# RWKV-7, MoBA and dilated attention: small TensorE products in merged steps, dilated outputs straight to their two parts

## The chip, the cores and the metric

One core of one Trainium2 chip runs the whole program: TensorE (in the profile PE for its matmuls and PEld for its weight loads), VectorE (DVE), ScalarE (ACT), GpSimd (POOL) and SyncE (SP), which issues most of the DMAs. The metric is device microseconds of one execution. Of the kernel before there are three timed runs, and one profiled execution beside them.

## The reference, cut to what matters

Four mixers stand in a row in a network of width 1024 on 512 tokens, each followed by a layer norm and an MLP. The change is in the first mixer (RWKV-7 beside MoBA attention) and in the second (dilated attention).

```python
def step(S, inp):                      # RWKV-7, 8 heads of 64
    r_t, w_t, k_t, v_t, a_t, b_t = inp
    sa = jnp.einsum('bhvk,bhk->bhv', S, a_t)
    S = S * w_t[:, :, None, :] + sa[..., None] * b_t[:, :, None, :] + v_t[..., None] * k_t[:, :, None, :]
    return S, jnp.einsum('bhvk,bhk->bhv', S, r_t)
...
p = jax.nn.softmax(s_all, axis=-1)     # MoBA, 4 heads of 128: with 2 blocks of 256 it is causal attention
...
for g, (span, dilation) in enumerate(((128, 1), (512, 4), (2048, 16))):   # dilated, 8 heads of 128
    o, l = _dilated_window_branch(q[:, g], k, v, span, dilation)
...
o = jnp.einsum('gbht,gbhtd->bhtd', wts, jnp.stack(outs, axis=0))
return o.reshape(B, T, C_WIDTH) @ w_out
```

The decay and the gates of RWKV-7 come from products with small matrices (`w_up`, `a_up`, `g_up`), and its output is normed by head, scaled and gated.

## The kernel before, in words

All matrices of weights are multiplied as two fp32r parts (a rounded value and what is left of it), three matmuls of 512 columns each: `gemm` in lines 276 to 278, `pjps` in lines 361 to 363. Everything small (all that the change touches in the first mixer) is in plain fp32, where each matmul of the program shows as two instructions in the trace.

The first mixer fills the first 355 us. RWKV-7 works on pairs of heads, p = 0 to 3, in chunks of 64 tokens (c = 0, 1 in each of four tiles t of 128 tokens). For each pair four generators make the work: `prep` (decay, keys, transposes to token order), `inner` (products within the chunks: `aak`, `arb`, `ark`), `core` (the inverse of a triangular matrix by doubling, then `tu`, the chunk's transition `mt` and contribution `ct`, the states, the output `yk`) and `tail` (norm and gate). MoBA has one generator per head. A small product takes a part of TensorE's array, given by `tile_position`: (64·h, 64·c) is the quarter of 64 rows and 64 columns that reads partitions 64·h and writes partitions 64·c.

The order of the work is made by a planner, `race`. Each generator yields (TensorE time, time until its result can be used) in estimated microseconds after each step; the planner takes the step that is ready first, and between steps it deals out triples of the big products from `stream`: after each step it owes 0.65 of that step's TensorE time in triples (`RACE_RWKV`), and pays as soon as over 0.6 us is owed. After that the framework's scheduler lays out each engine's queue, roughly in that order, and puts in all waits. The engines' queues run in order.

PSUM has eight banks. Two hold the big products. The other six are one ring (`K.mps`) for all small products of all generators: a step takes a bank when its matmuls start and gives it back when ACT or DVE has read it out.

In the steps that the change touches, the kernel before handles the two heads of a pair, or the two halves c of the chunks, one after the other: one bank, 8 to 24 matmuls, a yield, then the read-out. Within such a step one of the two coordinates of `tile_position` stays the same, or both change together.

The dilated attention (790 to 1080 us) works through eight heads in a second planner run (`RACE_DIL`, 0.5), with a bank `po` for a head's whole output. At the head's end ACT copies `po` to `yT` in token order, and `split` makes the two fp32r parts of that head, `ys[0]` and `ys[1]`, which the out-projection (`early`) reads:

```python
nc.scalar.copy(yT[:, h, :].rearrange("p (t i r) -> p t r i", t=NT, r=4), po.rearrange("p (t r i) -> p t r i", t=NT, r=4))
at[0] = h + 1
yield 0, 0.6
K.split(ys[0][:, h], ys[1][:, h], yT[:, h])
```

Lines that the prediction speaks of: 472 and 478 (`pw`, `pa`), 452 (transposes), 564 (`pp` of `inner`), 591 (`pp` of `core`, 32 columns), 652 (`pg`), 663 (`ptu`), 680 to 682 (`pmc`), 698 (`pqt`), 737 (`py2`), 878 to 904 (MoBA), 1325 to 1327 (dilated output), 1277 (dilated scores) and 1770 (a product of another mixer that the change leaves alone).

Of the kernel before, what the change touches and what calls it, by code (L numbers as in the profile page):

```python
# [18 lines left out]
P = 128  # L19
T = 512  # L20
# [382 lines left out]
def rwkv(K, ctx, x, win, first, par_d, wup_d, gup_d, yT, heads, done, load, more):  # L403
# [61 lines left out]
    def prep(p, R):  # L465
# [11 lines left out]
        pa = K.mps("pa")  # L477
        nc.tensor.matmul(pa, lhsT=wup[64:128, cs], rhs=wa[64:128, :], start=True, stop=True)
        yield 0.85, 0.85
# [60 lines left out]
        for dst, src in ((bk, bt), (kk_tm, kt), (v_tm, zv)):  # L540
            ps = tmaj(src)
            yield 0.45, 0.6
            nc.scalar.copy(dst.rearrange("p t c -> p (t c)"), ps)
        R.update(at=at_, bt=bt, kt=kt, rt=rt, wc=wc, bk=bk, kk=kk_tm, v=v_tm)

    def inner(p, R, Z):

        while "v" not in R or p and not state.get(f"core{p - 1}"):
            yield None
        rhs = sp.tile([P, 8, 2, 64], F32, name="rhs")  # L550
        ps = tmaj(R["at"])
        yield 0.45, 0.6
        nc.scalar.copy(
            rhs.rearrange("p (h t) w v -> p t h w v", h=2)[:, :, :, 0, :], ps.rearrange("p (t h v) -> p t h v", t=NT, h=2)
        )
        Z["rhs"] = rhs
        for name, l, r, m in (("aak", "kt", "at", "mus"), ("arb", "bt", "rt", "mui"), ("ark", "kt", "rt", "mui")):
            o = sp.tile([P, 8, 64], F32, name=name)
            for h in range(2):
                ps = K.mps("pp")  # L560
                for t in range(NT):
                    for c in range(2):
                        s = slice(t * P + 64 * c, t * P + 64 * c + 64)
                        nc.tensor.matmul(
                            ps[64 * c : 64 * c + 64, 64 * t : 64 * t + 64], lhsT=R[l][64 * h : 64 * h + 64, s],
                            rhs=R[r][64 * h : 64 * h + 64, s], start=True, stop=True, tile_position=(64 * h, 64 * c),
                        )
                yield 0.65, 0.65
                nc.vector.tensor_tensor(
                    o[:, 4 * h : 4 * h + 4, :], ps[:, 0:256].rearrange("p (t c) -> p t c", t=NT),  # L570
                    cn(m).unsqueeze(1).to_broadcast([P, NT, 64]), op=ALU.mult,
                )
            Z[name] = o
            yield 0, 0.4

    def core(p, R, Z):
# [6 lines left out]
        for h in range(2):  # L583
            r = slice(64 * h, 64 * h + 64)
            ps = K.mps("pp32")
            for t in range(NT):
                for w in range(2):
                    for q in range(4):
                        i = t * P + 32 * q
                        j = i if w == 0 else t * P + 64 * (q // 2)  # L590
                        nc.tensor.matmul(
                            ps[32 * q : 32 * q + 32, 128 * w + 32 * t : 128 * w + 32 * t + 32], lhsT=at_[r, i : i + 32], rhs=bt[r, j : j + 32],
                            start=True, stop=True, tile_position=(64 * h, 32 * q),
                        )
            yield 1.1, 1.1
            pv = ps[:, 0:256].rearrange("p (w t c) -> p w t c", w=2, t=NT)
            nc.vector.tensor_tensor(a32[:, 4 * h : 4 * h + 4, :], pv[:, 0], cn("m32sl").unsqueeze(1).to_broadcast([P, NT, 32]), op=ALU.mult)
            nc.scalar.copy(a10[:, 4 * h : 4 * h + 4, :], pv[:, 1])
# [59 lines left out]
        for h in range(2):  # L658
            pt = K.mps("ptu").rearrange("p (t w v) -> p t w v", t=NT, w=2)
# [6 lines left out]
            yield 1.0, 1.0  # L666
# [7 lines left out]
        for c in range(2):  # L674
            r = slice(64 * c, 64 * c + 64)
            ps = K.mps("pmc").rearrange("p (w t v) -> p w t v", w=2, t=NT)
            for t in range(NT):
                for h in range(2):
                    o = slice(64 * h, 64 * h + 64)
                    nc.tensor.matmul(ps[o, 1, t], lhsT=bk[r, t, o], rhs=tu[r, 1, t, h], start=True, stop=False, tile_position=(64 * c, 64 * h))  # L680
                    nc.tensor.matmul(ps[o, 1, t], lhsT=kk_tm[r, t, o], rhs=v_tm[r, t, o], start=False, stop=True, tile_position=(64 * c, 64 * h))
                    nc.tensor.matmul(ps[o, 0, t], lhsT=tu[r, 0, t, h], rhs=bk[r, t, o], start=True, stop=True, tile_position=(64 * c, 64 * h))
            yield 1.9, 1.9
            nc.vector.tensor_tensor(ct[:, :, c, :], ps[:, 1], bc(wct[:, :, c], 64), op=ALU.mult)
            nc.scalar.copy(mt_[:, :, c, :], ps[:, 0])
# [7 lines left out]
        for c in range(2):  # L693
            r = slice(64 * c, 64 * c + 64)
            ps = K.mps("pqt")[:, 0:256].rearrange("p (t l) -> p t l", t=NT)
            for t in range(NT):
                for h in range(2):
                    nc.tensor.matmul(
                        ps[64 * h : 64 * h + 64, t], lhsT=tu[r, 0, t, h, :], rhs=arb[r, 4 * h + t, :], start=True, stop=True,
                        tile_position=(64 * c, 64 * h))  # L700
            yield 0.65, 0.65
            nc.vector.tensor_tensor(Q[:, :, c, :], ps, R["rt"].rearrange("p (t c l) -> p t c l", t=NT, c=2)[:, :, c], op=ALU.add)
# [29 lines left out]
        for h in range(2):  # L732
            r = slice(64 * h, 64 * h + 64)
            ps = K.mps("py2")[:, 0:256].rearrange("p (t v) -> p t v", t=NT)
            for t in range(NT):
                for c in range(2):
                    nc.tensor.matmul(
                        ps[64 * c : 64 * c + 64, t], lhsT=Q[r, t, c, :], rhs=st[r, 2 * t + c, :], start=True, stop=True,
                        tile_position=(64 * h, 64 * c))
            yield 0.65, 0.65  # L740
            nc.vector.tensor_tensor(yk[:, :, h, :], yk[:, :, h, :], ps, op=ALU.add)
# [4 lines left out]
    def tail(p, R):  # L746
# [27 lines left out]
        yield 0.45, 0.6  # L774
        yo = sp.tile([P, T], F32, name="yo", tag="sqy")
        nc.scalar.activation(yo, pyt, AF.Identity, scale=pc("lg", p), bias=pc("lb", p))
        pgt = K.mps("pgt")
        nc.tensor.matmul(pgt, lhsT=gup[:, 0, cs], rhs=wa_["zg0"], start=True, stop=False)
        yield 0.85, 0.85
        nc.tensor.matmul(pgt, lhsT=gup[0:32, 1, cs], rhs=wa_["zg1"][0:32], start=False, stop=True)  # L780
        nc.vector.tensor_tensor(yo, yo, yT[:, p, :], op=ALU.add)
        yield 0.85, 0.85
# [49 lines left out]
def moba(K, ctx, c0, rope_d, yT, done):  # L832
# [20 lines left out]
    def head(h, R):  # L853
# [15 lines left out]
        pv = K.mps("mopv")  # L869
        for t in range(NT):  # L870
            nc.tensor.transpose(pv[:, t * P : t * P + P], vt[:, t * P : t * P + P], ident)
        yield 0.45, 0.6
        nc.scalar.copy(v.rearrange("p t d -> p (t d)"), pv)
        pr = []
        for t in range(NT):
            n = P * (t + 1)
            ps = K.mps("mosc")
            nc.tensor.matmul(ps[:, 0:n], lhsT=q[:, t * P : n], rhs=k[:, 0:n], start=True, stop=True)
            yield 0.2 * (t + 1), 0.6
            nc.vector.tensor_tensor(ps[:, t * P : n], ps[:, t * P : n], K.c("caus"), op=ALU.add)  # L880
            st = s2.tile([P, 4], F32, name="mstat")
            nc.vector.tensor_reduce(st[:, 0:1], ps[:, 0:n], axis=AX.X, op=ALU.max)
            nc.vector.tensor_scalar(st[:, 1:2], st[:, 0:1], -scale, None, op0=ALU.mult)
            p_ = sp.tile([P, n], F32, name=f"mp{t}")
            yield 0, 0.6
            nc.scalar.activation(p_, ps[:, 0:n], AF.Exp, scale=scale, bias=st[:, 1:2], accum_out=st[:, 2:3])
            yield 0, 0.6
            nc.vector.reciprocal(st[:, 3:4], st[:, 2:3])
            nc.vector.tensor_scalar(p_, p_, st[:, 3:4], None, op0=ALU.mult)
            pr.append(p_)  # L890
        yT_ = yT[:, 4 + h, :]
        po = K.mps("mopo")
        for b in range(NT):
            n = T - P * b
# [3 lines left out]
            yield 0.11 * (NT - b), 0.4  # L898
            pT = s2.tile([P, T], F32, name="mpt")[:, 0:n]
            (nc.scalar.copy if b % 2 else nc.vector.tensor_copy)(pT, pt[:, 0:n])  # L900
            yield 0.6, 0.6
            nc.tensor.matmul(po[:, b * P : T], lhsT=v[:, b, :], rhs=pT, start=b == 0, stop=b == NT - 1)
            yield 0.2 * (NT - b), 0.4
# [311 lines left out]
def dilated(K, ctx, S, x, win, rope_d, yT, ys, w_out):  # L1215
# [42 lines left out]
    def head(h, L):  # L1258
# [25 lines left out]
        po = L.acc("dipo")  # L1284
        ps = score(0)
        yield 0.7, 0.8
        for t in range(NT):
# [10 lines left out]
            yield (0.9 if t < NT - 1 else 0), 0.9  # L1298
# [30 lines left out]
        yield 0, 0.6  # L1329
        K.split(ys[0][:, h], ys[1][:, h], yT[:, h])  # L1330
        have.add(h)

# [860 lines left out]
def program(tc, A):  # L2193

    nc = tc.nc
    with ExitStack() as top:
# [46 lines left out]
        with ExitStack() as c:  # L2243
# [154 lines left out]
```

## Time and profile before

| | |
|---|---|
| median of 3 runs | 2176.72 us (2176.64 to 2177.35) |
| the profiled execution | 2178.79 us, its span 2177.0 us |
| mean granted TensorE clock | 0.991 of full |
| PE busy | 2133.3 us, 98% |
| DVE busy | 1214.7 us, 56% |
| ACT busy | 791.9 us, 36% |
| POOL busy | 181.3 us, 8% |

The span runs from the first to the last instruction; the execution has 1.8 us around it. A busy PE is a PE with at least one matmul on its way: matmuls overlap, and a row of the timeline merges neighbouring instructions of one line into one row with their count. How long a group holds TensorE is therefore read from start to start.

### The profile page before, as it was taken

The page shows a single profiled execution, that of the slowest core. Times are in us where ns is not written, and L with a number is a line of the kernel's source. Part 1 is how long each engine was busy: PE and PEld are TensorE (multiplying, and loading weights), DVE is VectorE, ACT ScalarE, POOL GpSimd, SP SyncE. Part 2 cuts the span into 40 slices and gives each one's busy share as a digit, 9 for nine tenths or more (in the row PEclk, how much of TensorE's full clock was granted, in tenths as well). Part 3 has the DMA queues.
Part 4 walks back from the last instruction along what each step waited for, and adds up shares of the span by engine and source line. Part 5 has one row for each costly group of instructions (what it writes and reads, how often), then busy time and mean ns, then how long its engine had stood idle before and what let it go on. Part 6 is the DMA issues. An engine that isn't in the chain of part 4 may idle for free.

```text
span 2177.0 us, 37054 instructions
## 1 busy us (share of the span) xinstructions
PE 2133.3 (98%) x15646; PEld 1699.1 (78%) x15646; DVE 1214.7 (56%) x2406; ACT 791.9 (36%) x1289; POOL 181.3 (8%) x268
## 2 busy tenths in 40 slices
PE   8999999999999999999999999999999999999998
PEld 6666667888887888787788888878677779888887
DVE  6675666764444655555574444466756466344445
ACT  4332324523232354444352233235524354222222
POOL 0011010061035400000000000010010000000000
PEclk9999999999999999999999999999989999999999
DMA  4111114333333332222243233314211232232321
GB/s 145 41 51 41 40 41 175 107 117 97 102 106 105 96 127 78 71 75 78 91 142 91 91 99 97 97 43 145 65 50 39 87 107 98 96 97 96 98 87 39
DMA packets 56182, 193.18 MB, mean 89 GB/s; under 512 B 8208, under 2 KB 8720, under 8 KB 55504
## 3 DMA queue, kind: packets, MB, share of 16 engines
q1 hardware_dynamic: 52480, 184.50, 26.2%
q0 software_dynamic: 3536, 6.32, 0.9%
q8 instruction: 122, 2.00, 0.4%
q14 instruction: 44, 0.36, 0.1%
HBM read 182.37 MB, written 8.39 MB: 88 GB/s over the span
## 4 chain that ended last, share of the span: by engine, by line
PE 88%; DVE 6%; ACT 2%; DMA 2%; issue 1%; POOL 0%; SPq 0%; DVEq 0%; ACTq 0%
PE gemm L276 8%; PE mlpo L361 7%; PE mlpo L363 7%; PE mlpo L362 7%; PE gemm L277 7%; PE gemm L278 7%; PE mlps L248 5%; PE mlps L249 5%; PE mlps L250 5%; PE ffg L249 2%; PE ffg L250 2%; PE ffu L249 2%; PE ffg L248 2%; PE ffu L250 2%; PE ffu L248 2%; PE pjps L361 1%
## 5 line engine op out<-in xcount | busy, mean ns | idle before, releaser
L227 ACT CAST wh<-wr 128x1024 fp32r<-128x1024 f32 (+1 forms) x311 | 323.7, 1043 | 766.0 <-PE mlpo L363 247.8
L229 DVE TENSOR_TENSOR wl<-wr,wh 128x1024 fp32r<-128x1024 f32 (+1 forms) x308 | 375.6, 1221 | 373.4 <-ACT wh L227 279.4
L276 PE MATMUL gemm<-acth,wh 128*128 128x512 f32 (+1 forms) x672 | 304.1, 453 | 9.5 <-ACT acth L237 6.3
L361 PE MATMUL mlpo<-wh,mlph 128*128 128x512 f32 x688 | 270.9, 394 | 0.0
L277 PE MATMUL gemm<-actl,wh 128*128 128x512 f32 (+1 forms) x672 | 269.4, 401 | 0.0
L363 PE MATMUL mlpo<-wh,mlpl 128*128 128x512 f32 x688 | 269.3, 392 | 0.0
L278 PE MATMUL gemm<-acth,wl 128*128 128x512 f32 (+1 forms) x672 | 268.1, 399 | 1.1 <-DVE wl L229 1.1
L362 PE MATMUL mlpo<-wl,mlph 128*128 128x512 f32 x688 | 268.8, 391 | 0.0
L248 PE MATMUL mlps<-acth,wh 128*128 128x512 f32 x448 | 175.7, 392 | 0.0
L249 PE MATMUL mlps<-actl,wh 128*128 128x512 f32 x448 | 175.5, 392 | 0.0
L250 PE MATMUL mlps<-acth,wl 128*128 128x512 f32 x448 | 175.3, 391 | 0.0
L276 PEld LDWEIGHTS gemm<-acth,wh 128*128 128x128 f32 (+1 forms) x672 | 127.1, 189 | 55.7 <-issue 18.3
L363 PEld LDWEIGHTS mlpo<-wh,mlpl 128*128 128x128 f32 x688 | 129.2, 188 | 29.5 <-DVE mlpl L238 0.2
L278 PEld LDWEIGHTS gemm<-acth,wl 128*128 128x128 f32 (+1 forms) x672 | 127.2, 189 | 31.0 <-DVE wl L229 1.9
L362 PEld LDWEIGHTS mlpo<-wl,mlph 128*128 128x128 f32 x688 | 129.2, 188 | 28.3
L361 PEld LDWEIGHTS mlpo<-wh,mlph 128*128 128x128 f32 x688 | 129.4, 188 | 28.1 <-ACT mlph L237 0.4
L277 PEld LDWEIGHTS gemm<-actl,wh 128*128 128x128 f32 (+1 forms) x672 | 128.0, 190 | 22.4 <-issue 5.3
L1039 DVE SCALAR_TENSOR_TENSOR xres<-xres,mlpo 128x512 f32<-128x512 f32 x120 | 82.1, 685 | 110.4 <-PE mlpo L363 109.6
L250 PEld LDWEIGHTS mlps<-acth,wl 128*128 128x128 f32 x448 | 84.1, 188 | 18.9
L248 PEld LDWEIGHTS mlps<-acth,wh 128*128 128x128 f32 x448 | 84.2, 188 | 18.5
L249 PEld LDWEIGHTS mlps<-actl,wh 128*128 128x128 f32 x448 | 84.1, 188 | 18.3
L237 ACT CAST mlph<-mlp 128x512 fp32r<-128x512 f32 x86 | 53.3, 620 | 86.2 <-DVE mlp L1115 61.0
(619 smaller groups left out, 3660.2 us busy)
## 6 DMA issues: line engine op xcount, KB each, us to landing
wr<-mlp_w SPq DMA_DIRECT2D x128, 512.0 KB, 3.7
wr<-ffn_w SPq DMA_DIRECT2D x66, 512.0 KB, 3.5
wr<-c_w_in SPq DMA_DIRECT2D x40, 512.0 KB, 3.6
wr<-ab_w_in SPq DMA_DIRECT2D x25, 512.0 KB, 3.5
wr<-w_in SPq DMA_DIRECT2D x24, 512.0 KB, 3.6
wr<-ab_w_out SPq DMA_DIRECT2D x8, 512.0 KB, 3.9
wr<-c_w_out SPq DMA_DIRECT2D x8, 512.0 KB, 3.7
wr<-w_out SPq DMA_DIRECT2D x8, 512.0 KB, 3.9
```

The source lines that it names most:

```text
L227: nc.scalar.copy(hi, raw)
L229: eng.tensor_tensor(lo, raw, hi.bitcast(F32), op=ALU.subtract)
L248: nc.tensor.matmul(ps, lhsT=hs, rhs=a, start=start and k == 0, stop=False)
L249: nc.tensor.matmul(ps, lhsT=hs, rhs=b, start=False, stop=False)
L250: nc.tensor.matmul(ps, lhsT=ls, rhs=a, start=False, stop=stop and k == n - 1)
L276: nc.tensor.matmul(ps[0:m], lhsT=h[:, 0:m], rhs=xh[:, k, :], start=k == 0, stop=False)
L277: nc.tensor.matmul(ps[0:m], lhsT=h[:, 0:m], rhs=xl[:, k, :], start=False, stop=False)
L278: nc.tensor.matmul(ps[0:m], lhsT=l[:, 0:m], rhs=xh[:, k, :], start=False, stop=k == n - 1)
L361: nc.tensor.matmul(ps, lhsT=a, rhs=h[:, c0 : c0 + n], start=start and k == 0, stop=False)
L362: nc.tensor.matmul(ps, lhsT=a, rhs=l[:, c0 : c0 + n], start=False, stop=False)
L363: nc.tensor.matmul(ps, lhsT=b, rhs=h[:, c0 : c0 + n], start=False, stop=stop and k == kt - 1)
L1039: self.K.nc.vector.scalar_tensor_tensor(xs, xs, f, ps, op0=ALU.mult, op1=ALU.add, accum_out=self.sums[:, t, c : c + 1])
```

## The change

In `prep`, `pw` and `pa` are computed in one step, in column halves by turns, and the three transposes are one step with three banks. In `inner`, both heads of a product are one step with two banks, with the head as the innermost loop, and the first product also takes the transposes of `at` into its step. In `core`, both halves of `pp32`, `ptu`, `pmc`, `pqt` and `py2` are one step each with two banks; in all but `ptu` the four (or eight) tile positions follow each other innermost. In `tail` the transposes and both gate products are one step. In MoBA the scores of t = 3, 0 and 1 are one step in two banks, those of t = 2 follow with the transposes of v; each softmax is issued as a whole, in the order 3, 0, 1, 2; each block's transposes are issued in the step of the matmul before. In the dilated attention the output goes from `po` to the two parts (ACT the first, DVE the second) without `yT`; the last head does so for each tile of 128 tokens as soon as it is done, and the yield after the output's matmuls is gone, its time counted in the next. The buffer `ymix` of that stage is gone. The yields' estimates follow the new steps.

```diff
@@ prep
-        pw = K.mps("pw")
-        nc.tensor.matmul(pw, lhsT=wup[0:64, cs], rhs=wa[0:64, :], start=True, stop=True)
-        yield 0.85, 0.85
+        pw, pa = K.mps("pw"), K.mps("pa")
+        for n in range(0, T, 256):
+            for r, ps in ((slice(0, 64), pw), (slice(64, 128), pa)):
+                nc.tensor.matmul(ps[:, n : n + 256], lhsT=wup[r, cs], rhs=wa[r, n : n + 256], start=True, stop=True)
+        yield 1.2, 1.2
...
-        for dst, src in ((bk, bt), (kk_tm, kt), (v_tm, zv)):
-            ps = tmaj(src)
-            yield 0.45, 0.6
+        turned = [tmaj(src) for src in (bt, kt, zv)]
+        yield 1.35, 1.5
+        for dst, ps in zip((bk, kk_tm, v_tm), turned):
             nc.scalar.copy(dst.rearrange("p t c -> p (t c)"), ps)
@@ inner
-            for h in range(2):
-                ps = K.mps("pp")
-                for t in range(NT):
-                    for c in range(2):
+            ps = [K.mps("pp") for h in range(2)]
+            for t in range(NT):
+                for c in range(2):
+                    for h in range(2):
                         s = slice(t * P + 64 * c, t * P + 64 * c + 64)
                         nc.tensor.matmul(
-                            ps[64 * c : 64 * c + 64, 64 * t : 64 * t + 64], lhsT=R[l][64 * h : 64 * h + 64, s],
+                            ps[h][64 * c : 64 * c + 64, 64 * t : 64 * t + 64], lhsT=R[l][64 * h : 64 * h + 64, s],
                             rhs=R[r][64 * h : 64 * h + 64, s], start=True, stop=True, tile_position=(64 * h, 64 * c),
                         )
-                yield 0.65, 0.65
+            yield (1.0 if pt is None else 1.45), 1.5
@@ core
+        pm2 = [K.mps("pmc").rearrange("p (w t v) -> p w t v", w=2, t=NT) for c in range(2)]
+        quads = [(c, h, slice(64 * c, 64 * c + 64), slice(64 * h, 64 * h + 64)) for c in range(2) for h in range(2)]
+        for t in range(NT):
+            for c, h, r, o in quads:
+                nc.tensor.matmul(pm2[c][o, 1, t], lhsT=bk[r, t, o], rhs=tu[r, 1, t, h], start=True, stop=False, tile_position=(64 * c, 64 * h))
+            for c, h, r, o in quads:
+                nc.tensor.matmul(pm2[c][o, 1, t], lhsT=kk_tm[r, t, o], rhs=v_tm[r, t, o], start=False, stop=True, tile_position=(64 * c, 64 * h))
+            for c, h, r, o in quads:
+                nc.tensor.matmul(pm2[c][o, 0, t], lhsT=tu[r, 0, t, h], rhs=bk[r, t, o], start=True, stop=True, tile_position=(64 * c, 64 * h))
+        yield 3.0, 3.0
...
@@ moba head
+        p3, p01 = K.mps("mosc"), K.mps("mosc")
+        score(3, p3)
+        score(0, p01[:, 0:P])
+        score(1, p01[:, P : 3 * P])
+        yield 1.4, 1.5
+        soft(3, p3)
+        p2, pv = K.mps("mosc"), K.mps("mopv")
+        score(2, p2[:, 0 : 3 * P])
...
+        soft(0, p01[:, 0:P])
+        yield 0, 0.6
+        soft(1, p01[:, P : 3 * P])
+        yield 0, 0.6
+        soft(2, p2[:, 0 : 3 * P])
+        yield 0, 1.5
@@ dilated head
+        def out(t, n):
+            src = po[:, t * P : (t + n) * P].rearrange("p (t r i) -> p t r i", t=n, r=4)
+            hi, lo = (y[:, h, t * P : (t + n) * P].rearrange("p (t i r) -> p t r i", t=n, r=4) for y in ys)
+            nc.scalar.copy(hi, src)
+            nc.vector.tensor_tensor(lo, src, hi.bitcast(F32), op=ALU.subtract)
...
-            yield 0.22 * (t + 1), 0.5
-        nc.scalar.copy(yT[:, h, :].rearrange("p (t i r) -> p t r i", t=NT, r=4), po.rearrange("p (t r i) -> p t r i", t=NT, r=4))
+            if h == 7:
+                out(t, 1)
+            sums = 0.22 * (t + 1)
+        if h < 7:
+            out(0, NT)
         at[0] = h + 1
-        yield 0, 0.6
-        K.split(ys[0][:, h], ys[1][:, h], yT[:, h])
         have.add(h)
+        yield sums, 1.3
```

## Rows read from the trace of the kernel before

**Rows 1.** The page, engines over the whole span: busy us, share, instructions.

```profile
PE 2133.3 (98%) x15646; PEld 1699.1 (78%) x15646; DVE 1214.7 (56%) x2406; ACT 791.9 (36%) x1289; POOL 181.3 (8%) x268
```

**Rows 2.** Windows of the first mixer: start:end, length, busy us of each engine, PEclk, DMA.

```profile
36.00:343.50 307.50, 304.48 (x5220) 211.95 (x5219) 199.99 (x446) 98.61 (x193) 27.17 (x23) 1.00 0.13 42
130.00:150.00 20.00, 20.00 (x505) 14.29 (x505) 18.24 (x29) 5.73 (x9) 2.27 (x2) 1.00 0.18 55
```

**Rows 3.** Waits of PE in 0 to 360 us: total, times, longest; first, third, last of seven.

```profile
PE gemm L276 <- ACT acth L237: 6.3, 1, 6.3
...
PE mopt L897 <- DVE mp L889: 1.1, 1, 1.1
...
PE pinv L629 <- DVE pm L619: 0.2, 1, 0.2
```

**Rows 4.** Timeline of PE, one group between big products: start, us, line, operation, shape, count.

```profile
107.99 0.40 PE L278 MATMUL gemm<-acth,wl 128*128 128x512 f32 x1
108.32 0.68 PE L737 MATMUL py<-state,qtb 64*64 64x64 f32 x16
108.93 0.50 PE L276 MATMUL gemm<-acth,wh 128*128 128x512 f32 x1
109.27 0.39 PE L277 MATMUL gemm<-actl,wh 128*128 128x512 f32 x1
109.50 0.40 PE L278 MATMUL gemm<-acth,wl 128*128 128x512 f32 x1
```

**Rows 5.** Timeline of PE, one group of each other kind.

```profile
58.67 1.12 PE L472 MATMUL pw<-rwa,wup 64*128 64x512 f32 x2
...
80.69 1.15 PE L652 MATMUL pg<-v_tm,aak 64*64 64x64 f32 x32
...
82.89 1.96 PE L663 MATMUL ptu<-rhs,ttc 64*64 64x128 f32 x32
...
85.60 0.33 PE L680 MATMUL pmc<-tu,b_tm 64*64 64x64 f32 x2
...
87.33 0.42 PE L277 MATMUL gemm<-actl,wh 128*32 128x512 f32 x1
...
111.76 0.76 PE L591 MATMUL pp<-tha,ld 64*32 64x32 f32 x64
...
155.34 1.09 PE L663 MATMUL ptu<-rhs,ttc 64*64 64x128 f32 x16
```

**Rows 6.** Timeline of PE, groups whose tiles lie side by side.

```profile
20.31 0.69 PE L472 MATMUL pw<-rwa,wup 64*128 64x512 f32 x1
20.32 0.69 PE L478 MATMUL pa<-rwa,wup 64*128 64x512 f32 x1
...
20.85 0.59 PE L478 MATMUL pa<-rwa,wup 64*128 64x512 f32 x1
...
803.14 0.43 PE L1277 MATMUL disc<-dz,dz 128*32 128x64 f32 x16
...
1538.45 0.76 PE L1770 MATMUL hgd<-hws 64*32 64x32 f32 x64
```

**Rows 7.** Groups of DVE and ACT in 0 to 355 us: count, busy us, mean ns, idle before.

```profile
L569 DVE TENSOR_TENSOR aak<-pp,consts 128x256 f32<-128x256 f32 x8 | 3.3, 414 | 0.6 <-PE pp L564 0.6
...
L886 ACT ACTIVATE mp<-mosc,mstat 128x128 f32<-128x128 f32 (+3 forms) x16 | 8.5, 528 | 31.4 <-DVE mstat L883 31.4
...
L543 ACT COPY v_tm<-ptm 128x512 f32<-128x512 f32 x4 | 2.4, 592 | 1.8 <-PE ptm L452 1.8
...
L598 ACT COPY a<-pp 128x128 f32<-128x128 f32 x8 | 2.1, 260 | 9.0 <-DVE a L597 9.0
```

**Rows 8.** Timeline of all engines at the end of the dilated attention.

```profile
1075.81 1.05 ACT L1327 COPY ymix<-dipo 128x512 f32<-128x512 f32 x1 [0.80 <-PE dipo L1325]
...
1077.56 0.50 PE L361 MATMUL pjps<-wh,acth 128*128 128x512 f32 x1 [1.79 <-ACT acth L237]
```

**Rows 9.** Window just after it, columns as in the windows above.

```profile
1078.30:1081.50 3.20, 3.20 (x9) 2.48 (x9) 1.71 (x5) 0.00 (x0) 0.00 (x0) 0.52 0.97 352
```

More of the change, by code (lines that the diff above doesn't have):

```diff
@@ L582, in core @@
         a10 = sp.tile([P, 8, 32], F32, name="a10")
-        for h in range(2):
-            r = slice(64 * h, 64 * h + 64)
-            ps = K.mps("pp32")
+        ps = [K.mps("pp32") for h in range(2)]
+        for w in range(2):
             for t in range(NT):
-                for w in range(2):
-                    for q in range(4):
+                for q in range(4):
+                    for h in range(2):
+                        r = slice(64 * h, 64 * h + 64)
                         i = t * P + 32 * q
@@ L657, in core @@
         tu = sp.tile([P, 2, NT, 2, 64], F32, name="tu")
-        for h in range(2):
-            pt = K.mps("ptu").rearrange("p (t w v) -> p t w v", t=NT, w=2)
+        pts = [K.mps("ptu").rearrange("p (t w v) -> p t w v", t=NT, w=2) for h in range(2)]
+        for h, pt in enumerate(pts):
             for t in range(NT):
@@ L673, in core @@
         wct = wc.rearrange("p (t c) -> p t c", c=2)
[L674 to L683, printed above, removed]
+        pm2 = [K.mps("pmc").rearrange("p (w t v) -> p w t v", w=2, t=NT) for c in range(2)]
[8 more added lines that the diff above has]
+        yield 3.0, 3.0
+        for c, ps in enumerate(pm2):
             nc.vector.tensor_tensor(ct[:, :, c, :], ps[:, 1], bc(wct[:, :, c], 64), op=ALU.mult)
@@ L692, in core @@
         nc.scalar.copy(st[:, 1, :], ctf[:, 0, :])
[L693 to L701, printed above, removed]
+        pq2 = [K.mps("pqt")[:, 0:256].rearrange("p (t l) -> p t l", t=NT) for c in range(2)]
+        for t in range(NT):
+            for c, h, r, o in quads:
+                nc.tensor.matmul(
+                    pq2[c][o, t], lhsT=tu[r, 0, t, h, :], rhs=arb[r, 4 * h + t, :], start=True, stop=True, tile_position=(64 * c, 64 * h))
+        yield 1.0, 1.0
+        for c, ps in enumerate(pq2):
             nc.vector.tensor_tensor(Q[:, :, c, :], ps, R["rt"].rearrange("p (t c l) -> p t c l", t=NT, c=2)[:, :, c], op=ALU.add)
@@ L731, in core @@
         nc.scalar.copy(yk, pi.rearrange("p (h t) v -> p t h v", h=2))
[L732 to L740, printed above, removed]
+        py2 = [K.mps("py2")[:, 0:256].rearrange("p (t v) -> p t v", t=NT) for h in range(2)]
+        for t in range(NT):
+            for h, c, r, o in quads:
+                nc.tensor.matmul(
+                    py2[h][o, t], lhsT=Q[r, t, c, :], rhs=st[r, 2 * t + c, :], start=True, stop=True, tile_position=(64 * h, 64 * c))
+        yield 1.0, 1.0
+        for h, ps in enumerate(py2):
             nc.vector.tensor_tensor(yk[:, :, h, :], yk[:, :, h, :], ps, op=ALU.add)
@@ L868, in head, with score, soft @@
         v = sp.tile([P, NT, P], F32, name="mv")
-        pv = K.mps("mopv")
+        pr = [None] * NT
+        def score(t, ps):
+            n = P * (t + 1)
+            nc.tensor.matmul(ps, lhsT=q[:, t * P : n], rhs=k[:, 0:n], start=True, stop=True)
+        def soft(t, ps):
+            n = P * (t + 1)
+            nc.vector.tensor_tensor(ps[:, t * P : n], ps[:, t * P : n], K.c("caus"), op=ALU.add)
+            st = s2.tile([P, 4], F32, name="mstat")
+            nc.vector.tensor_reduce(st[:, 0:1], ps, axis=AX.X, op=ALU.max)
+            nc.vector.tensor_scalar(st[:, 1:2], st[:, 0:1], -scale, None, op0=ALU.mult)
+            pr[t] = sp.tile([P, n], F32, name=f"mp{t}")
+            nc.scalar.activation(pr[t], ps, AF.Exp, scale=scale, bias=st[:, 1:2], accum_out=st[:, 2:3])
+            nc.vector.reciprocal(st[:, 3:4], st[:, 2:3])
+            nc.vector.tensor_scalar(pr[t], pr[t], st[:, 3:4], None, op0=ALU.mult)
@@ L875, in head @@
[L875 to L884, printed above, removed]
-            yield 0, 0.6
[L886 to L890, printed above, removed]
+        soft(0, p01[:, 0:P])
```

69 lines of the change are left out of this document (35 added, 34 removed).

## The prediction

> **What bounds the kernel now.** Read the page's busy shares first: PE stands at 98% of the span [rows 1]. Then take the first mixer alone by windows: from 36 to 343.5 us PE is busy for 304.5 of 307.5 us, DVE for 200.0, ACT for 98.6 [rows 2]. The waits of PE there are seven kinds; the longest, 6.3 us, is the start, and the next sort is 1 to 2 us [rows 3]. So TensorE's own time sets the end of this stage. But "busy" only says that some matmul is on its way, so the third view is PE's timeline, start to start. One big product follows another after 0.23 us (109.27 to 109.50). A group of 16 small matmuls in between starts 0.33 us after the last big one and holds TensorE from 108.32 to 108.93, 0.61 us; the next big one then takes 0.34 instead of 0.23 [rows 4]. So each visit to the small tiles costs 0.10 us going in and 0.10 coming out, 0.20 together, whatever it holds. A row's length ends 0.07 us after the next start (108.32 + 0.68 against 108.93), so I take 0.07 off where I use a length.
>
> A group's own time: 16 matmuls of 64 columns on two tiles take 0.61, 32 (L652, also on two) 1.15 - 0.07 = 1.08 [rows 4, 5]. Eight rounds more cost 0.47 us, so a round is 0.0585 us, and 0.14 us is fixed. Two tiles work in one round.
>
> **Part 1: four tiles in a round.** With both heads (or both c) innermost, four quarters of the array are addressed by turns. Does a round then hold four? Two rows speak for it. 16 matmuls of 64 columns on four column tiles (L1277) take 0.43 - 0.07 = 0.36 us, against 0.61 on two. And `pw` and `pa`, which differ in rows alone, ran together once: started at 20.31 and 20.32, the last instruction 0.59 long from 20.85, so both in 21.44 - 0.07 - 20.31 = 1.06 us [rows 6], where one alone takes 1.12 - 0.07 = 1.05 [rows 5]. No row has rows and columns both in quarters, so the ends are four per round and still two per round; I take four.
>
> - `pp` of `inner` (3 products), `pqt`, `py2`, for four pairs of heads: 20 times two groups become one. Before 2 x (0.61 + 0.20) = 1.62. After: 32 matmuls, 8 rounds, 0.61 + 0.20 = 0.81. Saved 20 x 0.81 = 16.2 us.
> - `pmc`, 4 times: a group of 48 holds 85.60 to 87.33 = 1.73 [rows 5], before 2 x 1.93 = 3.86. After: 96 matmuls, 24 rounds, 0.14 + 1.40 + 0.20 = 1.74. Saved 4 x 2.12 = 8.5.
> - `pw` and `pa`: three of the four pairs of heads run apart (as at 58.67 in [rows 5]), 2 x 1.25 = 2.50; after, as at 20.31, 1.06 + 0.20. Saved 3 x 1.24 = 3.7. Column halves load weights twice as often; nothing is charged, since in [rows 6] a second load already goes beside the first's columns.
> - `ptu` keeps two tiles. Its group of 16 takes 1.02, one of 32, as the first pair already has, 1.89 [rows 5]. Saved 3 x (2.44 - 2.09) = 1.0.
> - `pp32`: 64 matmuls on four tiles take 0.69 [rows 5], 64 on eight tiles (L1770) also 0.69 [rows 6]. Eight tiles give nothing: the floor is (0.69 - 0.14) / 64 = 8.6 ns a matmul, below the 0.0585 / 4 = 14.6 that four quarters need. Merged: 128 x 8.6 ns + 0.14 + 0.20 = 1.44 for 1.78. Saved 4 x 0.34 = 1.4.
>
> Sum 30.8 us; some groups lie against another small group and pay no way in or out, say three, 0.6. Leaves 30.2.
>
> The Trainium skill (TensorE: Matmul & The Clock Gate, "Wait — 56ns, not 53.3ns?") says that matmuls never start closer than about 25 ns. By that, 32 would take 0.94 us and 96 take 2.54, and the two first items come to 9.6 + 4.5 instead of 16.2 + 8.5. The 8.6 ns of [rows 5] contradict it, so I don't use it.
>
> **Part 2: what is given back.** Merged steps read out two or three banks after all their matmuls instead of one during the other's. A half is 0.41 us on DVE [rows 7]; where the big products fill the gap it costs nothing, but at the end, where `core` of the last pair runs nearly alone, three steps pay 0.41 each: 1.2. DVE has 18.24 of 20 us in 130 to 150 [rows 2]; there at most 1.76 us can go, and about as much would: 0 to 1 lost. The small waits of PE outside the start (under 6 us) may double in the denser queue: 3. I charge 5 of a range from 0 (cover holds) to 15 (half). The first mixer gains 25.2.
>
> MoBA, transposes, `pyt` with `pgt`: these are full-array fp32 products that need no visit to small tiles, and their matmuls stay as many. I cost them at 0. Below: the one wait for `mp` could vanish, -1.1 [rows 3]. Above: a softmax issued whole puts DVE's reciprocal behind ACT's exponential, 16 of 0.53 us [rows 7]; if DVE stood still for each and PE felt it, +8.5. DVE has a third of the stage free, so nearer to 0.
>
> **Part 3: dilated.** For the last head the out-projection waits for two ACT instructions in a row, the copy of 1.05 us and the cast that PE's row names, and PE stands for 1.79 [rows 8]. Behind the gap the granted clock is 0.52 over 3.2 us [rows 9], the lower of its two levels (1.2 of 2.4 GHz), so another 3.2 x 0.48 = 1.5 is lost. After: three quarters of the head are out before, and the last waits for one ACT copy of a quarter, 0.26 us by its like [rows 7], beside nine matmuls of the other quarters (9 x 0.23 = 2.1). So both go: 3.3 us; if the clock falls all the same, 1.8. For the other seven heads ACT loses an instruction of about 1 us each, off the path: 0. DVE now reads the bank itself and holds `po` longer; the next head writes it only after its first score and softmax: 0.
>
> **Sum.** 25.2 + 3.3 = 28.5. The profiled execution took 2177.0 + 1.8 = 2178.8, so 2150.3 for its like; the median of the runs lies 2.1 below it (2176.72): 2148.2. I forecast 2148.
>
> **The rivals.**
> A, four quarters don't share a round. For: no row shows it. Against: columns and rows each do. The 20 merges save 20 x (1.62 - 1.28) = 6.8, `pmc` 4 x (3.86 - 3.15) = 2.8; the rest stands at 6.1. 15.7 + 3.3 - 2 of losses = 17: 2178.8 - 17 - 2.1 = 2160.
>
> B, the read-outs take over: PE's time shrinks and the stage goes at the pace of DVE and ACT. For: DVE at 91% in 130 to 150. Against: 65% over the stage (200 of 307.5), 72% after. If each of the 34 merged pairs waits for one more half, 34 x 0.41 = 14: 30.2 - 14 + 3.3 = 19.5, 2178.8 - 19.5 - 2.1 = 2157. This is also a rule of the Trainium skill (TensorEngine Tiling (Array Packing), "PSUM Bottleneck"): tiling speeds up the products, not the copies out of PSUM, which may then bound.
>
> C, slower: the ring of six banks runs dry. MoBA now holds up to four banks at once, `prep` takes three, `inner` three, the others two; a merged step waits until ACT has given back a bank, and behind that step stands everything on PE, big products too. About 11 steps for each of four pairs and 4 for each head are 60. A copy is 0.59 us [rows 7]; with half of another ahead of it, 0.89 a step: 53 us, 2178.8 + 53 - 33.5 - 2.1 = 2196. It turns the sign from 33.5 / 60 = 0.56 us a step. Against: the big products have banks of their own and can be laid between, and PE now waits for almost nothing.
>
> **How the numbers follow.** Forecast 62%, A 14%, B 14%, C 6%, other ways of no gain 4%. With nothing lost and the MoBA wait gone, 30.8 + 3.3 + 1.1 = 35.2: 2141.5, the lower end, 2141. The upper holds A and B with some us of MoBA: 2166. The forecast's own range is 2142 to 2155. 0.2%, about what can be told from no change, is 4.4 us; faster than that 0.90 (forecast, A, B), same 0.04, slower 0.06.
>
> **What would show it.** A group of 32 of L564's successor holding TensorE for about 0.61 us, `pmc` about 1.55 for 96, `pw` with `pa` 1.06: part 1. If 32 take 1.08, A. PE's waits for ACT or DVE in the first 350 us well over 12 us, with small products as the waiting ones: B, or C when what is awaited is a bank's reader. The stage's end: the long run of big products that starts at 355 us should start near 330. At the end of dilated, no gap of 1.8 us and no low clock behind it. Wrong would be: a time above 2166, or a first mixer that ends early while the rest gets longer.

## The result and the profile after

The changed kernel takes 2150.02 us (median of 4 runs, 2149.44 to 2151.2) beside 2176.68 us of the kernel before (4 runs): a ratio of 0.988, 95% interval 0.9867 to 0.9894, 26.7 us faster. The forecast was 2148, its range 2141 to 2166. The profiled execution took 2150.12 us with a span of 2148.3; that of before, 2178.79, stands 2.1 above its median, so the two traces differ by 28.7.

The engines of the page after, beside [rows 1]: PE has 34 us less, DVE and ACT about what they had.

```profile
PE 2099.4 (98%) x15662; PEld 1680.8 (78%) x15662; DVE 1212.2 (56%) x2409; ACT 786.1 (37%) x1284; POOL 183.6 (9%) x268
```

The stages, as windows (start:end, length, busy us of PE, PEld, DVE, ACT, POOL with counts, PEclk, DMA), first of the kernel before: the first mixer from 36 us to the end of its last small product, the projection until the MLP starts, the dilated attention, from its end to the mixers of the last block, these mixers, and the last MLP.

```profile
36.00:355.10 319.10, 315.56 (x5267) 218.81 (x5265) 209.06 (x476) 101.71 (x200) 28.36 (x25) 1.00 0.14 43
355.10:395.90 40.80, 39.97 (x182) 32.26 (x181) 28.84 (x52) 20.10 (x28) 0.00 (x0) 1.00 0.65 228
801.00:1075.80 274.80, 273.53 (x1766) 218.88 (x1765) 155.64 (x382) 123.99 (x220) 0.00 (x0) 1.00 0.24 73
1075.80:1466.80 391.00, 387.24 (x1789) 319.79 (x1789) 201.68 (x339) 129.86 (x184) 8.32 (x4) 1.00 0.31 98
1466.80:1801.40 334.60, 324.03 (x2607) 247.02 (x2607) 213.09 (x485) 153.92 (x289) 15.09 (x30) 0.96 0.24 81
1801.40:2169.50 368.10, 366.35 (x1744) 307.60 (x1744) 164.70 (x223) 103.75 (x148) 0.00 (x0) 1.00 0.27 87
```

The same stages of the changed kernel:

```profile
36.00:333.40 297.40, 286.61 (x5276) 202.66 (x5274) 203.03 (x475) 103.11 (x201) 29.86 (x25) 1.00 0.15 47
333.40:375.30 41.90, 40.37 (x183) 32.69 (x183) 29.20 (x52) 18.92 (x26) 0.00 (x0) 1.00 0.62 222
781.40:1053.70 272.30, 272.30 (x1764) 218.66 (x1764) 158.97 (x385) 120.02 (x216) 0.00 (x0) 1.00 0.24 74
1053.70:1442.30 388.60, 385.97 (x1792) 318.90 (x1790) 201.70 (x339) 128.36 (x183) 8.33 (x4) 1.00 0.31 98
1442.30:1774.40 332.10, 322.03 (x2606) 245.73 (x2606) 212.99 (x485) 154.03 (x289) 15.10 (x30) 0.97 0.25 82
1774.40:2141.00 366.60, 364.80 (x1744) 306.10 (x1744) 164.83 (x223) 103.70 (x148) 0.00 (x0) 1.00 0.27 88
```

Subtract line from line. The first mixer is 21.7 us shorter: PE's busy time falls by 28.95, its idle time (length less busy) grows from 3.5 to 10.8, by 7.3. The projection behind it gives 1.1 back. The dilated attention is 2.5 shorter, what follows it 2.4, and the last two stages are 2.5 and 1.5 shorter, though no instruction of theirs changed. With +1.0 for the MLP and the start of the dilated stage between 375 and 781 us these sum to 28.5 of 28.7.

The groups of part 1, beside [rows 4, 5]: the timeline of PE (start, us, line, operation, shape, count).

```profile
39.99 1.29 PE L590 MATMUL pp<-tha,ld 64*32 64x32 f32 x128
41.21 0.50 PE L278 MATMUL gemm<-acth,wl 128*128 128x512 f32 x1
...
58.18 0.48 PE L474 MATMUL pw<-rwa,wup 64*128 64x256 f32 x1
...
59.25 0.50 PE L276 MATMUL gemm<-acth,wh 128*128 128x512 f32 x1
...
79.17 0.34 PE L679 MATMUL pmc<-tu,b_tm 64*64 64x64 f32 x8
...
80.73 0.50 PE L278 MATMUL gemm<-acth,wl 128*128 128x512 f32 x1
...
97.58 0.40 PE L278 MATMUL gemm<-acth,wl 128*128 128x512 f32 x1
97.91 0.69 PE L735 MATMUL py<-state,qtb 64*64 64x64 f32 x32
98.53 0.50 PE L276 MATMUL gemm<-acth,wh 128*128 128x512 f32 x1
```

Start to start, 32 matmuls on four quarters hold TensorE for 0.62 us (0.61 forecast), `pmc`'s 96 for 1.56 (1.54), `pw` with `pa` 1.07 (1.06), `pp32`'s 128 for 1.22 (1.24); the way in is still 0.33 (97.58 to 97.91).

The waits of PE in 0 to 340 us, beside [rows 3] (in total, times, longest), the first four:

```profile
PE gemm L276 <- ACT acth L237: 6.7, 1, 6.7
PE pyt L771 <- DVE yk L767: 3.2, 2, 1.6
PE pinv L615 <- DVE yc L633: 1.4, 2, 1.2
PE pinv L615 <- DVE yc L604: 1.3, 1, 1.3
```

The start is nearly as it was. Behind it most of the waits are for VectorE; `pyt` waited 1.7 us before the change too, the waits for `yc` are new. In another 1.9 us PE waited for nothing that the profile shows. What stood ahead of two of them (timeline of DVE): a reciprocal ahead of the `yc` for which PE waits 1.2 us, to 133.47; and the norm's chain of eleven small operations, one after the other, with nothing else on DVE, ahead of the `yk` for which PE waits 1.6 us, to 330.88:

```profile
129.70 3.35 DVE L521 RECIPROCAL n<-n 128x512 f32<-128x512 f32 x1
132.96 0.36 DVE L633 TENSOR_TENSOR yc<-pinv,yc 128x256 f32<-128x256 f32 x1
...
328.03 0.17 DVE L151 TENSOR_SCALAR rs_i<-gs 128x8 int32<-128x8 int32 x1
...
330.04 0.69 DVE L767 TENSOR_TENSOR yk<-yk,grs 128x512 f32<-128x512 f32 x1
```

The end of the dilated attention, beside [rows 8] (timeline):

```profile
1052.66 1.05 PE L1351 MATMUL dipo<-dpt,dv 128*128 128x128 f32 x8
1053.47 0.48 PE L361 MATMUL pjps<-wh,acth 128*128 128x512 f32 x1
1053.76 0.38 ACT L1307 CAST acth<-dipo 128x128 fp32r<-128x128 f32 x1 [1.41 <-PE dipo L1351]
...
1054.17 0.40 DVE L1308 TENSOR_TENSOR actl<-dipo,acth 128x128 fp32r<-128x128 f32 x1 [2.28 <-ACT acth L1307]
```

PE goes from the last output on into the projection of the quarters that are out already, and the last quarter's two parts are made beside it. The window behind, where [rows 9] had 0.52 over 3.2 us, has 1.00:

```profile
1053.70:1057.00 3.30, 3.30 (x16) 2.68 (x15) 2.25 (x6) 0.38 (x1) 0.00 (x0) 1.00 0.66 160
```

### The profile page after: what moved, and what is told of

Its sections match the earlier page's. It is cut to its first block, busy times and chain, and to the rows that moved or that the text cites. A ratio compares the mean times of both kernels' runs of the same rounds, so it can differ in the third digit from the quotient of the medians.

```text
span 2148.3 us, 37089 instructions
## 1 busy us (share of the span) xinstructions
PE 2099.4 (98%) x15662; PEld 1680.8 (78%) x15662; DVE 1212.2 (56%) x2409; ACT 786.1 (37%) x1284; POOL 183.6 (9%) x268
## 3 DMA queue, kind: packets, MB, share of 16 engines
q1 hardware_dynamic: 52480, 184.50, 26.7%
## 4 chain that ended last, share of the span: by engine, by line
PE 87%; DVE 7%; ACT 3%; DMA 1%; issue 1%; POOL 0%; SPq 0%; DVEq 0%; ACTq 0%; POOLq 0%
PE gemm L276 8%; PE mlpo L361 7%; PE mlpo L363 7%; PE mlpo L362 7%; PE gemm L277 7%; PE gemm L278 7%; PE mlps L248 5%; PE mlps L249 5%; PE mlps L250 5%; PE ffg L249 2%; PE ffu L249 2%; PE ffg L250 2%; PE ffu L248 2%; PE ffu L250 2%; PE ffg L248 2%
## 5 line engine op out<-in xcount | busy, mean ns | idle before, releaser
L276 PE MATMUL gemm<-acth,wh 128*128 128x512 f32 (+1 forms) x672 | 297.1, 442 | 9.9 <-ACT acth L237 6.7
```

Of the source, the lines that this page charges most:

```text
L276: nc.tensor.matmul(ps[0:m], lhsT=h[:, 0:m], rhs=xh[:, k, :], start=k == 0, stop=False)
```

## The experiments

Each was timed against the kernel before on its own chip; medians of before there were 2172.43 (the first four), 2174.2 (the next four), 2175.53 (the next three) and 2173.83 (the last).

**Order inside the merged step.** The steps stay merged (one yield, the same banks), but one head (or half) is laid wholly before the other, so two quarters go by turns and then the other two.

```diff
@@ inner; pmc, pqt and py2 likewise
-            for t in range(NT):
-                for c in range(2):
-                    for h in range(2):
+            for h in range(2):
+                for t in range(NT):
+                    for c in range(2):
```

> The merged steps stay (same banks, same yields), but inside pp of inner, pmc, pqt and py2 one head (or one half c) comes wholly before the other, so only two quarters of the array are addressed by turns. Theory (the order is what lets four quarters share a round): a group of 32 takes 16 rounds, 1.08 us instead of the 0.625 of the changed kernel, pmc of 96 some 3 us instead of 1.56; 20 x 0.455 + 4 x 1.45 = 15 us more: 2165. Rival (what counts is that the visits are merged; TensorE looks ahead far enough to run the second head beside the first): groups of 32 at about 0.63 us and 2150.

2161.49 us (2159.3 to 2162.58), ratio 0.9945, 0.993 to 0.9959. Its timeline of PE:

```profile
42.53 0.97 PE L558 MATMUL pp<-ld,e 64*64 64x64 f32 x32
43.43 0.50 PE L276 MATMUL gemm<-acth,wh 128*128 128x512 f32 x1
...
79.78 0.33 PE L680 MATMUL pmc<-tu,b_tm 64*64 64x64 f32 x4
...
82.55 0.50 PE L278 MATMUL gemm<-acth,wl 128*128 128x512 f32 x1
```

The same 32 matmuls now take 0.90 us and the 96 take 2.77. Twenty groups at 0.28 more and four at 1.21 more are 10.4, and the last small product stands 10.4 us later (343.8 against 333.4). The theory holds and the rival (merging alone is what counts) falls; in the groups the size is under the forecast because matmuls of the second half already run beside the last of the first (0.90, not 1.08). So by the groups, 10.4 of the 28.5 us are the order alone. By the times it is more, 12 to 16 us: this run is 10.9 us faster than before on its chip, the whole change 26.7 and, timed again below, 22.8. In the merged order the two banks alternate along with the quarters, and no run parts the two. Against the banks as the cause stands `pg` (L652 in [rows 5]): its two quarters write one bank and still share a round.

**Each part alone.** The kernel before with one part of the change. Of the diff ahead, the first takes all of `prep`, `inner`, `core` and `tail`, the second all of MoBA's head, the third all of the dilated head and the buffer that goes with it; a line of each stands for them.

```diff
@@ the first: prep, inner, core, tail
+            ps = [K.mps("pp") for h in range(2)]
@@ the second: moba head
+        p3, p01 = K.mps("mosc"), K.mps("mosc")
@@ the third: dilated head
+            nc.scalar.copy(hi, src)
```

> The kernel before with the changed RWKV-7 part alone (MoBA and dilated as before). Theory: nearly all of the gain, the first mixer's long run of big products starts near 333 us, as in the whole change, and only the 3 us of dilated are missing: 2153 to 2156. Rival (MoBA's softmaxes in a row carry part of it, or cost part of it): 2158 or more, or under 2150, with the first mixer's end elsewhere than 333.

Part 1 alone: 2167.91 us (2162.74 to 2171.65), ratio 0.997, 0.9958 to 0.9982.

> The kernel before with the changed MoBA alone. Theory: nothing, since its products are on the full array and keep their count: 2175 to 2178. Rival 1 (each softmax issued whole blocks DVE's queue): up to 8 us more, 2185. Rival 2 (it frees the chain at the first mixer's end): 2 to 5 us less, 2172 to 2175.

Part 2 alone: 2183.09 us (2181.27 to 2184.57), ratio 1.0044, 1.0031 to 1.0057. It is slower.

> The kernel before with the changed dilated part alone (and without that stage's ymix). Theory: the gap of 1.79 us before the out-projection's last head and the low clock behind it go: 3.3 us less, 2173.4; the run up to 790 us as before. Rival (the clock falls all the same, or another low stretch comes instead): 1.8 us less, 2175.

Part 3 alone: 2171.03 us (2168.0 to 2175.53), ratio 0.9996, 0.9986 to 1.0005.

The three sum to -4.5 + 10.7 - 1.4 = +4.8 us; together they give -26.7, and -22.8 when timed again below. So the parts are not independent. Part 1 alone, waits of PE in 0 to 350 us, and windows:

```profile
PE mopt L894 <- DVE mp L886: 3.4, 3, 2.0
PE pyt L771 <- DVE yk L767: 2.5, 2, 1.9
PE pyt L771 <- DVE s5pw L2075: 2.3, 1, 2.3
```

```profile
36.00:347.10 311.10, 294.83 (x5275) 207.13 (x5274) 210.00 (x476) 102.78 (x200) 29.75 (x25) 0.97 0.15 49
347.10:388.00 40.90, 40.15 (x184) 32.54 (x183) 28.34 (x52) 19.83 (x27) 0.00 (x0) 1.00 0.55 192
...
256.00:265.00 9.00, 7.06 (x88) 3.77 (x89) 7.43 (x16) 2.90 (x4) 3.52 (x3) 0.73 0.21 59
271.00:279.00 8.00, 6.67 (x211) 4.86 (x212) 2.31 (x6) 0.85 (x2) 0.00 (x0) 0.79 0.02 4
329.00:346.00 17.00, 10.89 (x29) 5.41 (x28) 8.62 (x30) 3.89 (x9) 1.19 (x2) 0.80 0.38 123
```

PE idles for 16.3 us of the mixer, 12.7 more than before and 5.5 more than with the whole change. It is also busy for 8.2 us more than with the whole change (294.83 against 286.61). For the most part that is the clock: around the longest waits it is 0.73 to 0.80, which costs 9 x 0.27 + 8 x 0.21 + 17 x 0.20 = 7.5 us, while over the whole change's mixer it reads 1.00. The two make this mixer 13.7 us longer, and the MLP starts 12.7 later (388.0 against 375.3; the starts of one and the same code lie up to 1 us apart in two profiles). So the work is gone about as costed; waits of MoBA's single steps (`mopt`, and `mopv` with 1.4) and of `pyt` and the slower clock around them eat it.

**The norm chain's estimate, in the whole change.** The planner is told that the norm's small operations in `tail` take 2.5 us, not 0.6. The changed kernel itself ran beside it.

```diff
@@ tail
         K.rsqrt(s2, rs, s2_, "grs")
-        yield 0, 0.6
+        yield 0, 2.5
```

> The changed kernel itself, so that the next three are compared with it on one chip. Theory: 2150 +- 1.5 us, 0.988 of the kernel before.

2151.37 us (2149.8 to 2155.74), ratio 0.99, 0.9883 to 0.9916. The time is as in the first timing; the gain is 22.8 us and not 26.7, since the kernel before ran faster here (2174.2), and the two intervals overlap.

> The changed kernel, with the chain of eleven small norm operations in tail() declared 2.5 us long to the planner of the race and not 0.6. Theory (part of the 30 us that TensorE no longer works in the first mixer is idle again because turns are laid into its queue while the norm chain on VectorE runs: two waits of 1.6 us at pyt): the two pyt waits go, 2148 us, idle of TensorE from 36 us to the end of the mixer falls from 10.8 us to about 8. Rival A (what is idle there is set by the chain and not by the place in the queue): no change, 2150 us. Rival B (later turns push the tail behind the last head of MoBA): 2152 to 2155 us.

2149.42 us (2146.68 to 2150.3), ratio 0.9889, 0.9872 to 0.9905. In the trace both waits of `pyt` are gone and idle time from 36 us to the last small product is 296.0 - 288.8 = 7.2 us:

```profile
36.00:332.00 296.00, 288.80 (x5287) 204.60 (x5285) 203.46 (x476) 104.30 (x203) 30.05 (x25) 1.00 0.16 48
```

In the trace the theory holds: idle time fell by 3.6, and the MLP starts at 370.1, 5.2 us sooner. In the times the 2 us lie within the overlap of the intervals, so as a gain it stays likely, not shown.

**Is VectorE short of time?** Two edits of the whole change: the reciprocal cut in four, and 16 copies moved to ScalarE (two of `tu` for each pair of heads, two of `pT` for each head of MoBA).

```diff
@@ prep, the first
-        nc.vector.reciprocal(n2, n2)
-        yield 0, 1.2
+        yield 0, 0.6
+        for i in range(0, T, P):
+            nc.vector.reciprocal(n2[:, i : i + P], n2[:, i : i + P])
+            yield 0, 0.9
@@ core and moba, the second
-                (nc.vector.tensor_copy if w else nc.scalar.copy)(tu[:, w, :, h, :], pt[:, :, w])
+                nc.scalar.copy(tu[:, w, :, h, :], pt[:, :, w])
-            (nc.scalar.copy if b % 2 else nc.vector.tensor_copy)(pT, pt[:, 0:n])
+            nc.scalar.copy(pT, pt[:, 0:n])
```

> The changed kernel, with the 3.35 us reciprocal of prep() cut in four of 128 columns, so that VectorE can do the small inverse's yc between two of them. Theory (VectorE's queue order makes the rest of the idle time): the waits for yc (1.4 us in all, longest 1.2) go, 2148.5 us. Rival (the wait is the length of the chain): no change, 2150 us; the cost of three more instructions on VectorE, some 0.1 us each per pair, lies beside TensorE's work.

2151.98 us (2148.33 to 2152.52), ratio 0.9896, 0.9881 to 0.9911: no change. The waits for `yc` went (0.2 us is left), another grew from 0.6 (waits of PE, 0 to 340 us), and the idle time is 9.2 us where it was 10.8:

```profile
PE pinv L631 <- DVE pm L621: 3.4, 3, 1.8
```

> The changed kernel, with the two copies of tu and the two of MoBA's pT that VectorE makes put on ScalarE: some 8 us less on VectorE, as much more on ScalarE, in the first mixer. Theory (VectorE's capacity has become a limit of the first mixer in part): 1 to 3 us faster, 2148 us. Rival (read-outs that go in turn on two engines matter more: a step's two copies now follow each other, 16 x 0.4 us on chains): slower by 2 to 5 us, 2153 us, since each chain grows by 0.4 us a step.

2149.94 us (2147.96 to 2152.41), ratio 0.9891, 0.9876 to 0.9905: no change, idle time 10.1. Neither the gain nor the loss came. DVE is busy for 6.1 us less in the mixer (196.9 against 203.0), and the waits for it hardly shrink, so its capacity does not make them. What does is only in part shown: the reciprocal stood ahead of `yc`, and with it in pieces that wait moved elsewhere; the last wait for `yk` is the length of the norm's chain, with nothing else on DVE.

**The norm chain's estimate, in each part alone.** If the waits of `pyt` make part 1 alone poor and part 2 alone slow, the same edit should mend both.

```diff
@@ tail, in part 2 alone and in part 1 alone
-        yield 0, 0.6
+        yield 0, 2.5
```

> Part 2 alone (MoBA's softmaxes in a row and its longer turns), with the norm chain of tail() declared 2.5 us long to the planner. Part 2 alone had been slower than the kernel before by 10.7 us, with two waits for yk (1.9 us and 3.4 us) and a stretch at 0.50 behind each. Theory (what part 2 costs alone are these waits and the low clock that follows them): both waits go, and with them 5.3 us of idle time and some 5 us of low clock: 2172 us, no slower than before. Rival (the end of the mixer is set by RWKV's chain, which MoBA's heads push back): the mixer ends as late as with part 2 alone, 2181 to 2184 us.

2184.92 us (2180.99 to 2197.63), ratio 1.0052, 1.0032 to 1.0073; the waits are as they were (36 to 375 us, in total, times, longest), that of 1.4 us at the projection too:

```profile
PE pyt L773 <- DVE yk L769: 6.4, 3, 3.4
```

> Part 1 alone (RWKV's merged steps), with the norm chain of tail() declared 2.5 us long. Part 1 alone had gained 4.5 us, with three waits for yk (0.6, 1.9 and 2.3 us) among 16.3 us of idle time from 36 to 347 us, and 20 us at 0.50 between 260 and 393 us. Theory (part 1 frees its 29 us in full, and idle time with the low clock behind it eats them): the three waits go (4.8 us) and two of the four stretches in the mixer (10.2 us at half speed, 5 us): about 2158 us. Rival (MoBA's heads in single steps set the end of the mixer at 347 us whatever RWKV's tails do): 2166 to 2168 us.

2167.11 us (2166.01 to 2172.3), ratio 0.9968, 0.9956 to 0.998; waits of 2.0 and 2.5 us for `pyt` stay. My theory fell in both, and the times are near the rivals'. That the longer estimate moves `pyt` only where there is something to lay in its place is my reading, and no run shows it.

**Longer estimates everywhere.** The whole change, the norm chain at 2.5, and all waits counted 1.1 times.

```diff
-RACE_RWKV = (0.65, 0.05, 0.9)
+RACE_RWKV = (0.65, 0.05, 1.1)
@@ tail
-        yield 0, 0.6
+        yield 0, 2.5
```

> The whole change, with the norm chain of tail() declared 2.5 us long and every wait of a chain counted 1.1 times by the planner instead of 0.9 times. With 154 to 166 big products left when the small work ends, the chains may grow by some 30 us before they set the end. Theory (what idle time is left in the mixer, 7.2 us with the longer tail alone, comes from turns laid too early): idle from 36 us to the end of the small work falls to 3 to 4 us, 2146 us. Rival (VectorE's own order makes these waits, at yc behind a reciprocal and behind the norm chain): they move and stay, 2150 us.

2152.1 us (2151.17 to 2152.86), ratio 0.9894, 0.9877 to 0.9911. Idle time is 10.1 us, not 3 to 4; a wait of 1.9 for `pyt` is back and `pinv` waits for other results. The rival holds: the waits move and stay.

**What makes part 2 alone late.** The timeline of PE of part 2 alone near the end of its mixer, right behind MoBA's last product (347.06): a step of RWKV's last chain, then projections; the next step of the chain comes 6.57 us later.

```profile
347.48 0.33 PE L719 MATMUL pst<-state,mt 64*64 64x64 f32 x4
347.75 0.50 PE L361 MATMUL pjps<-wh,acth 128*128 128x512 f32 x1
...
354.32 0.34 PE L708 MATMUL py<-tu,arb 64*64 64x64 f32 x4
...
369.46 1.09 PE L773 MATMUL pyt<-consts,yk 128*128 128x128 f32 x4 [3.39 <-DVE yk L769]
...
374.93 0.50 PE L361 MATMUL pjps<-wh,acth 128*128 128x512 f32 x1 [1.43 <-ACT acth L237]
```

The stream of projections had been unable to give anything while the last head's steps ran, so the planner's debt had grown, and was paid in one row. In the experiment that debt is dropped. The planner's other runs (the dilated attention and the last block's mixers) get the same line.

```diff
@@ race
                     waits.clear()
                     continue
+                owed = 0
```

> Part 2 alone, with one line more in the planner: while the stream of big products can give nothing, the debt that small work owes it is dropped. In part 2 alone the last head's turns and products stood in a row where the stream was blocked, and the planner then laid 27 projections (6.6 us) in a row ahead of the next step of RWKV's last chain, which was the last to end; at its end nothing was left to lay beside the norm chain (pyt waited 3.4 us, then the projection 1.4 us, each with a stretch at 0.50 behind it). Theory (this order makes the end of part 2 alone late): the six steps of RWKV's last chain stand together again, both waits shrink to under 1.5 us in sum, and the time falls by 5 to 6 us to 2178 us, still slower than before. Rival (the chain is late for what happened before 330 us): the waits stay, 2183 to 2185 us.

2170.46 us (2167.28 to 2180.97), ratio 0.999, 0.9977 to 1.0003. Its timeline at the same place:

```profile
347.82 0.33 PE L720 MATMUL pst<-state,mt 64*64 64x64 f32 x4
347.99 0.33 PE L709 MATMUL py<-tu,arb 64*64 64x64 f32 x4
...
348.80 0.50 PE L362 MATMUL pjps<-wh,acth 128*128 128x512 f32 x1
```

The chain's steps stand together, the wait of 3.4 at `pyt` is gone (one of 1.9 is left at the projection), and the MLP starts at 398.2 us instead of 406.0. The theory holds for the order and its cost, though the wait left is longer than the 1.5 forecast. The gain of some 12 us is twice the forecast, because the line also acts later: the last block's mixers take 324.5 us where they take 330.7 in part 2 alone. Of the 10.1 us by which the MLP of part 2 alone started late (406.0 against 395.9), 7.8 were thus the row of projections and what followed it; 2.3 are left.

The whole change with the longer norm chain and without the debt, to which these runs point, was not run.

## Why the prediction was right, and where it was not

**The bound** was read rightly: TensorE's own time set the first mixer's end, and taking 29 us of it away ended the mixer 21.7 us sooner.

**Part 1** was right in its mechanism and in each group to 0.02 us. The sum, 30.2, measured as 28.95 of busy time. Rival A was wrong about four quarters; the first experiment shows the price that it would have had if they had been addressed in another order. The Trainium skill (TensorE: Matmul & The Clock Gate, "Wait — 56ns, not 53.3ns?") gives about 25 ns as the least distance of two matmuls. The trace does not agree: on eight tiles by turns, 128 of them in 1.22 us are under 10 ns each.

**What is given back** was put at 5 and measured as 7.3, inside its 0 to 15. The form was half right. Idle time did triple, but hardly on read-outs of pairs (0.4 us, at `pmc`), and DVE did not fill up: it is busy for 68% of the mixer, 203.0 of 297.4 us, where 72% was forecast. The waits are for results that stand behind a longer instruction or at the end of a chain of short ones on DVE. Rival B, capacity of the read-outs, is not borne out. The same goes here for the Trainium skill's rule (TensorEngine Tiling (Array Packing), "PSUM Bottleneck") that copies out of PSUM may bound after tiling: with 16 copies moved from VectorE to ScalarE the time stayed (2149.94 beside 2151.37). Rival C had nothing: the waits for which the profile names a cause are for data, not for a bank's reader.

**MoBA at 0** is the step that failed: "I cost them at 0", with -1.1 and +8.5 as ends. Its value depends on what runs beside it. On top of part 1 it gives 12.7 us of the first mixer, far below the lower end: it takes away `mopt`'s and `mopv`'s waits and the low clock around them. Alone it costs 10.7 by the times (6.7 to 12.4) and 10.1 by the start of the MLP, at or above the upper end, for the most part (7.8) through the planner's order. I priced it as instructions, which it hardly changes, and not as waits beside a queue that part 1 makes denser. The two errors met in one number: part 1 with 25.2 was credited with what, alone, it doesn't give (388.0 against 395.9, 7.9 us).

**Part 3**, 3.3, was right in its place and short in size. The gap of 1.79 and the low clock behind it went, and the stage behind is 2.4 us shorter. Another 2.5 lie inside the stage, which had been put at 0: before, PE had waited 1.2 us there for `dz`, which ACT evacuates, and this wait is gone; the rest is busy time that no row places. So "off the path: 0" for ACT's seven copies of 1 us is likely the wrong term; no run parts these copies from the new order of the planner's steps. Part 3 alone has the same 272.3 us there with PE busy throughout; its time alone, 1.4 us less than before, cannot be told from none.

**The sum** hit to 2 us because the misses cancel: mixer and projection -20.6 for -25.2, part 3 -4.9 for -3.3, and some -3 in stages that the change doesn't touch. About half of these 3 us is the clock: added up over windows of 2 us, the lower level costs 11.9 us in the last block's mixers before and 10.2 after, 1.7 and none in the last MLP, 1.7 and 3.4 from the first MLP to the dilated stage. These runs show no part of the change in it. That the forecast came so close is luck: its terms were off by 4.6 us one way and by 1.6 and 3 the other, and the runs of the kernel before alone spread from 2169 to 2180 us.

What stays open: whether part 1's loss when alone is at bottom the waits or the clock, since no run removes one without the other. The loss itself is steady: the mean granted clock was 0.987 to 0.992 in nine runs of part 1 alone, 0.991 to 0.994 in eight of the whole change.

## What to carry to other kernels

Small products on different quarters of TensorE shared their time here, but for some 0.18 us a group, only where neighbouring instructions addressed different quarters: make the tile position the innermost loop, and compute the saving from start to start, with the way in and out as a term. Once the bound engine's work shrinks, price every chain beside it anew: a restructuring that changes no instruction count can be worth more than its own queue shows, or cost it alone, so time the parts together before dropping one. Where a planner deals out filler work by debt, look for stretches in which the filler is blocked: what is paid back in one row can land ahead of the chain that ends last.

## What the runs showed of the hardware

- Order alone made the difference between two quarters and four at a time: 32 matmuls of 64 columns on the same four quarters take 0.62 us by turns and 0.90 in two halves; 96 take 1.56 and 2.77. The two halves overlap by only some 0.18 us (1.08 expected without it, 0.90 measured), an estimate of three rounds of 0.0585 us.
- Idle time of the same length did not always bring the lower clock. In part 2 alone, and in part 2 alone with the longer norm chain, PE stands for 1.90 us ahead of the same `pyt` (to 203.56 and 203.83 us). The windows round it, in this order, read 0.81 and 1.00:

```profile
201.00:210.00 9.00, 7.10 (x171) 4.24 (x170) 4.89 (x13) 0.78 (x1) 0.66 (x1) 0.81 0.01 2
201.00:210.00 9.00, 7.10 (x180) 4.32 (x178) 5.84 (x14) 0.78 (x1) 0.93 (x1) 1.00 0.01 2
```

- Two executions of one kernel differ in this too: with the whole change the clock is 1.00 over 260 to 275 us in the first profile and 0.89 in the second, behind a wait of 1.57 and 1.64 us for the same `yk`. So a stretch at the lower clock in one trace need not be a property of the kernel.
- A reciprocal of 128x512 holds VectorE for 3.35 us, where a product of two such tiles takes 0.68; in four pieces it is 0.915 us each, 3.66 together.
